# Windowed attention on one core: the first loads issued at once by GpSimd, a quarter of the first q over SyncE, TensorE's loop without alignment

## Chip, core and metric

One core of one Trainium2 chip. The metric is the device time of one execution in microseconds (us). A single core has no second die to compare with, so only the spread of the runs themselves says what noise is. The experiments came in five sets, each on another chip, and beside each set nine runs of the kernel before were taken: these 45 runs lie between 942.4 and 944.6 us, and their five medians between 942.6 and 943.1 us. Differences of less than about 0.5 us between two medians are therefore not read as anything here.

## The reference

Attention inside windows of 64 rows, in float32 arrays of 4 x 4096 x 1536:

```python
logits = np.einsum('bnwd,bnud->bnwu', q_w, k_w) * D ** -0.5     # nw = 64 windows of W = 64 rows
logits = logits - logits.max(axis=-1, keepdims=True)
attn = np.exp(logits)
attn = attn / attn.sum(axis=-1, keepdims=True)
out = np.einsum('bnwu,bnud->bnwd', attn, v_w)
```

Every byte of q, k and v is read once and every byte of out written once: 302 MB and 101 MB.

## The kernel before

The kernel works in 32 units of 512 rows. For each unit GpSimd issues three loads (q, k, v), which cast float32 to float16 on the way and land in one of two landing buffers each, and one store. It copies a landed tile to its working place, tells TensorE through a semaphore, and requests the same tile of two units later. So loads are queued two units, about 55 us, ahead. The parts that matter:

```python
def hand_over(x, u, dst, m, g):                # GpSimd, for each tile of units 1 to 31
    gp.wait_ge(landed[x][u % NL], ...)         # the transfer has landed
    gp.wait_ge(m, u)                           # the working tile is free
    gp.tensor_copy(out=dst[...], in_=landing[x][u % NL][...]).then_inc(c_l, 1)
    ...
    gp.sem_inc(g, 1)                           # TensorE may go
    request(x, u + NL)                         # next load into the landing buffer
# [...]
# start: q of unit 0 comes as float32 over SyncE in four pieces, GpSimd casts it
for lo, hi, c0, c1, s in (
    (0, 1, 0, D // 2, d_r0), (0, 1, D // 2, D, d_r1), (1, 2, 0, D, d_r2), (2, SLOTS, 0, D, d_r3)
):
    nc.sync.dma_start(out=outs[0][:, lo:hi, c0:c1], in_=raw[:, lo:hi, c0:c1]).then_inc(s, 16)
nc.gpsimd.wait_ge(d_r0, 16)
nc.gpsimd.affine_select(out=ident[:, :], ...).then_inc(i_p, 1)
load("k", 0, k16, d_k0)
load("v", 0, v16, d_v0)
for i in range(SLOTS):
    nc.gpsimd.wait_ge((d_r1, d_r2, d_r3, d_r3)[i], 16)
    nc.gpsimd.tensor_copy(out=q16[:, i, :], in_=outs[0][:, i, :]).then_inc(c_q, 1)
    if i == 1:
        request("q", 1)
for x, u in (("k", 1), ("v", 1), ("q", 2), ("k", 2), ("v", 2)):
    request(x, u)
# [...]
with nc.Fori(0, N, engines=OrderedEngineSet([PE]), head_slot={PE: 0}):   # loop head at slot 0 of a fetch block
    tensor_unit()
# [...]
for u in range(1, N):
    hand_over("q", u, q16, m_q, g_q)
    hand_over("k", u, k16, m_k, g_k)
    gp.wait_ge(m_q, u + 1)
    store(u - 1)
    hand_over("v", u, v16, m_v, g_v)
```

The softmax here doesn't subtract the row's maximum and nothing guards it: scores larger than these inputs give would overflow.

## Time and profile before

| | before |
|---|---|
| time, median of the first three runs | 943.18 us (942.78 to 943.63) |
| span of the profiled run | 941.3 us |
| busiest compute engine | TensorE, 70% |

How to read the views: PE is TensorE (PEld its weight loads, PEq its sequencer), DVE VectorE, ACT ScalarE, POOL GpSimd. DMA queue q0 carries what GpSimd issues, q1 what SyncE issues. A line of the timeline has its start in us, its length in us, the engine, the line of the source, the operation, what it wrote and read, and in brackets how long the engine was idle before it and what ended that. In the view of narrow stretches the last two columns are the mean busy share of the 16 DMA engines and the GB/s that they moved, counted in SBUF bytes. The prediction below shows the lines of the kernel before.

### The profile page before, as it was taken

What the parts mean: (1) busy time and instruction counts of PE and PEld (TensorE: products, weight loads), DVE (VectorE), ACT (ScalarE), POOL (GpSimd) and SP (SyncE); (2) the same over time, 40 slices, a digit from 0 to 9 for tenths busy, and PEclk for the clock granted to TensorE, in tenths of its full rate; (3) what the DMA queues carried; (4) which work ended last, traced back from release to release, by engine and by line L of the source; (5) the groups of instructions that cost most, each with busy time, mean ns of one, the idle gap of its engine ahead of it and who ended that gap; (6) DMA issues with size and microseconds to landing.
All of it is one profiled execution on the core that took longest, in us unless ns stands there. A gap on an engine that the chain in (4) does not pass through costs nothing. (4 is left out here: it accounts for less than half of the span.)

```text
span 941.3 us, 11422 instructions
## 1 busy us (share of the span) xinstructions
PE 655.5 (70%) x4096; PEld 395.4 (42%) x3456; DVE 279.8 (30%) x453; ACT 335.9 (36%) x642; POOL 340.4 (36%) x228
## 2 busy tenths in 40 slices
PE   1888676866777768677677686776767768667672
PEld 1555344533455334444244543444433445334440
DVE  0433322333313323133332233322333223332231
ACT  1444433333333333333433324433333323343332
POOL 4344333344333443333423334333343333433221
PEclk9999978889878888888888878978888888898887
DMA  9999999999999999999999999999999999999998
GB/s 247 216 217 281 254 247 281 282 281 263 239 280 283 281 271 232 280 282 281 277 234 273 281 281 282 238 264 282 280 282 248 253 284 279 281 257 245 283 297 366
DMA packets 27084, 253.35 MB, mean 269 GB/s; under 512 B 2112, under 2 KB 2112, under 8 KB 10688
## 3 DMA queue, kind: packets, MB, share of 16 engines
q0 software_dynamic: 26208, 246.95, 100.0%
q1 hardware_dynamic: 864, 6.29, 1.7%
q14 instruction: 10, 0.08, 0.0%
q8 instruction: 2, 0.03, 0.0%
HBM read 301.99 MB, written 100.66 MB: 428 GB/s over the span
## 5 line engine op out<-in xcount | busy, mean ns | idle before, releaser
L157 PE MATMUL lt<-xq,xk 128*128 128x256 f16 x1536 | 215.5, 292 | 0.0
L145 PE MATMUL tp<-ident,k 128*128 128x128 f32 x768 | 149.1, 339 | 84.8 <-PEq L211 74.7
L294 POOL COPY v<-vl 128x3072 f32<-128x3072 f32 x31 | 85.2, 2747 | 296.0 <-DMA vl<-in_v_dram 296.0
L157 PEld LDWEIGHTS lt<-xq,xk 128*128 128x128 f16 x1536 | 159.6, 104 | 33.0
L145 PEld LDWEIGHTS tp<-ident,k 128*128 128x128 f32 x768 | 115.5, 176 | 104.7 <-issue 102.1
L145 PE MATMUL tp<-ident,q 128*128 128x128 f32 x768 | 109.7, 289 | 71.1 <-DVE xq L220 37.0
L220 ACT COPY xk<-tp 128x512 f32<-128x512 f32 x96 | 59.3, 618 | 264.0 <-ACTq L211 264.0
L186 PEld LDWEIGHTS <-et 128*128 128x128 f16 x384 | 34.5, 108 | 283.0 <-issue 277.2
L145 PEld LDWEIGHTS tp<-ident,q 128*128 128x128 f32 x768 | 89.2, 148 | 111.0 <-issue 110.4
L220 DVE COPY xk<-tp 128x512 f32<-128x512 f32 x96 | 66.5, 693 | 229.0 <-DVEq L211 229.0
L294 POOL COPY q<-ql 128x3072 f32<-128x3072 f32 x31 | 85.0, 2742 | 109.9 <-DMA ql<-in_q_dram 109.9
L294 POOL COPY k<-kl 128x3072 f32<-128x3072 f32 x31 | 85.2, 2747 | 107.6 <-DMA kl<-in_k_dram 107.6
L113 PE MATMUL o<-v,et 128*128 128x512 f16 x384 | 113.6, 440 | 0.0
L113 PE MATMUL sp<-ones,et 128*128 128x1 f16 x256 | 25.7, 170 | 116.6 <-PEq L211 114.3
L262 ACT ACTIVATE et<-lt,zeros 32x128 f16<-32x128 f32 x256 | 92.0, 360 | 39.4 <-ACTq L211 36.2
L220 ACT COPY xq<-tp 128x512 f32<-128x512 f32 x96 | 59.8, 623 | 122.1 <-ACTq L211 122.1
L249 DVE TENSOR_SCALAR out<-o,rs 128x512 f32<-128x512 f32 x128 | 91.1, 747 | 33.6 <-DVEq L211 29.6
L273 ACT ACTIVATE out<-tp,rs 128x512 f32<-128x512 f32 x64 | 44.0, 687 | 139.7 <-ACTq L211 112.9
L220 DVE COPY xq<-tp 128x512 f32<-128x512 f32 x96 | 66.3, 690 | 90.0 <-DVEq L211 89.8
L113 PE MATMUL tp<-v,et 128*128 128x512 f16 x256 | 91.9, 446 | 0.0
L239 DVE RECIPROCAL rs<-sp 128x2 f32<-128x2 f32 x64 | 10.7, 168 | 264.8 <-DVEq L211 264.8
L113 PE MATMUL lt<-v,et 128*128 128x512 f16 x128 | 58.3, 456 | 0.0
(21 smaller groups left out, 224.0 us busy)
## 6 DMA issues: line engine op xcount, KB each, us to landing
out_dram<-out POOLq DMA_DIRECT2D x31, 3072.0 KB, 61.8
ql<-in_q_dram POOLq DMA_DIRECT2D x31, 1536.0 KB, 54.9
kl<-in_k_dram POOLq DMA_DIRECT2D x31, 1536.0 KB, 54.9
vl<-in_v_dram POOLq DMA_DIRECT2D x31, 1536.0 KB, 54.9
out_dram<-out SPq DMA_DIRECT2D x2, 1536.0 KB, 9.7
out<-in_q_dram SPq DMA_DIRECT2D x1, 1536.0 KB, 13.9
k<-in_k_dram POOLq DMA_DIRECT2D x1, 1536.0 KB, 13.1
v<-in_v_dram POOLq DMA_DIRECT2D x1, 1536.0 KB, 19.7
```

What stands on the lines that cost most here:

```text
L113: return nc.tensor.add_instruction(mybir.InstMatmult(name=nc.get_next_instruction_name(), engine=PE, ins=[low(rhs), low(w)], outs=[low(o)] ...
L145: ins = nc.tensor.transpose(tps[g % 2][:, r, j, :], pairs[:, c * P : (c + 1) * P], ident[:, :])
L157: ins = nc.tensor.matmul(lts[h][:, r, :, :], lhsT=halves(xk, c)[:, r, h, :, w], rhs=halves(xq, c)[:, :, h, :, w], start=(c == 0 and w == 0 ...
L186: ld = nc.tensor.ldweights(w)
L220: copy(out=dst, in_=tps[g % 2][:, :, :, :]).then_inc(f_c[g % 4], 1)
L239: ve.reciprocal(out=rs[:, n : n + R], in_=sp[:, n : n + R]).then_inc(n_d, 1)
L249: ins = ve.tensor_scalar_mul(scaled(u, n, j), bank(n, j), scalar1=rs[:, n : n + 1])
L262: ins = sc.activation(ets[h][s, :, :, s], lts[h][s, :, :, s], EXP, bias=zeros[s, 0:1], scale=scale)
L273: ins = sc.activation(scaled(u, n, j), bank(n, j), COPY, bias=0.0, scale=rs[:, n : n + 1])
L294: gp.tensor_copy(out=dst[:, :, :].bitcast(FP32), in_=landing[x][u % NL][:, :, :].bitcast(FP32)).then_inc(c_l, 1)
```

## The change

The intent: nothing at the start should wait for anything it does not need. GpSimd no longer waits for the first piece of q before it issues k and v; three quarters of q come by a casting load of GpSimd itself, only a quarter over SyncE, which saves three of four casts. The alignment of TensorE's loop is dropped in the same step.

```diff
-        for lo, hi, c0, c1, s in (
-            (0, 1, 0, D // 2, d_r0), (0, 1, D // 2, D, d_r1), (1, 2, 0, D, d_r2), (2, SLOTS, 0, D, d_r3)
-        ):
-            nc.sync.dma_start(out=outs[0][:, lo:hi, c0:c1], in_=raw[:, lo:hi, c0:c1]).then_inc(s, 16)
+        first = rows(qf, 0, SLOTS, SLOTS)
+        nc.sync.dma_start(out=outs[0][:, 0, :], in_=first[:, 0, :D]).then_inc(d_r0, 16)
+        nc.gpsimd.dma_start(
+            out=q16[:, 1:, :].rearrange("p r d -> p (r d)"), in_=first[:, 0, D:]
+        ).then_inc(d_q0, 16)
+        load("k", 0, k16, d_k0)
         ...
-        nc.gpsimd.wait_ge(d_r0, 16)
         nc.gpsimd.affine_select(...)
-        load("k", 0, k16, d_k0)
         load("v", 0, v16, d_v0)
-        for i in range(SLOTS):
-            nc.gpsimd.wait_ge((d_r1, d_r2, d_r3, d_r3)[i], 16)
-            nc.gpsimd.tensor_copy(out=q16[:, i, :], in_=outs[0][:, i, :]).then_inc(c_q, 1)
-            if i == 1:
-                request("q", 1)
-        for x, u in (("k", 1), ("v", 1), ("q", 2), ("k", 2), ("v", 2)):
-            request(x, u)
+        for u in (1, 2):
+            for x in "qkv":
+                request(x, u)
+        nc.gpsimd.wait_ge(d_r0, 16)
+        nc.gpsimd.tensor_copy(out=q16[:, 0, :], in_=outs[0][:, 0, :]).then_inc(c_q, 1)
         ...
-        with nc.Fori(0, N, engines=OrderedEngineSet([PE]), head_slot={PE: 0}):
+        with nc.Fori(0, N, engines=OrderedEngineSet([PE])):
         ...
-        sy.wait_ge(c_q, SLOTS)
-        sy.sem_inc(g_q, 1)
+        sy.wait_ge(c_q, 1)
+        sy.sem_inc(g_q, 1)._wait_ge(d_q0, 16)
```

More of the change, by code (lines that the diff above doesn't have):

```diff
@@ L72 @@
     sp = ps("sp", [P, 4])
-    d_r0, d_r1, d_r2, d_r3, d_k0, d_v0 = (
-        sem(n) for n in ("d_r0", "d_r1", "d_r2", "d_r3", "d_k0", "d_v0")
-    )
+    d_r0, d_q0, d_k0, d_v0 = (sem(n) for n in ("d_r0", "d_q0", "d_k0", "d_v0"))
     landed = {x: [sem(f"d_{x}{i + 1}") for i in range(NL)] for x in "qkv"}
@@ L302 @@
     with tc.tile_critical(no_gpsimd_drain=True):
-        raw = rows(qf, 0, SLOTS, SLOTS).rearrange("p h (r d) -> p (h r) d", d=D)
-        for lo, hi, c0, c1, s in (
-            (0, 1, 0, D // 2, d_r0), (0, 1, D // 2, D, d_r1), (1, 2, 0, D, d_r2), (2, SLOTS, 0, D, d_r3)
-        ):
-            nc.sync.dma_start(
-                out=outs[0][:, lo:hi, c0:c1], in_=raw[:, lo:hi, c0:c1]
-            ).then_inc(s, 16)
+        first = rows(qf, 0, SLOTS, SLOTS)
[4 more added lines that the diff above has]
+        load("k", 0, k16, d_k0)
         nc.vector.memset(ident[:, :], 0.0).then_inc(i_d, 1)
         nc.gpsimd.wait_ge(i_d, 1)
-        nc.gpsimd.wait_ge(d_r0, 16)
         nc.gpsimd.affine_select(
```

## The prediction

> **What bounds the kernel now.** I read the page first, then the DMA queues, the GpSimd timeline, narrow stretches of the start and of the end, and last the waits of TensorE. The page says at once which resource never rests:
>
> ```profile
> PE 655.5 (70%) x4096; PEld 395.4 (42%) x3456; DVE 279.8 (30%) x453; ACT 335.9 (36%) x642; POOL 340.4 (36%) x228
> ...
> DMA  9999999999999999999999999999999999999998
> ...
> q0 software_dynamic: 26208, 246.95, 100.0%
> q1 hardware_dynamic: 864, 6.29, 1.7%
> q14 instruction: 10, 0.08, 0.0%
> ...
> HBM read 301.99 MB, written 100.66 MB: 428 GB/s over the span
> ```
>
> The row of the DMA engines is at nine tenths or more in 39 of 40 slices, from the first to the last but one, while the busiest compute engine has 30% to spare. The GB/s row counts bytes as SBUF sees them: a load that casts float32 to float16 counts half of what it reads from HBM. So 216 GB/s in such a row means 432 GB/s read from HBM, and the row's ups and downs (216 to 283) are the mix of loads and stores, not idle time.
>
> The GpSimd timeline gives the beat, because GpSimd copies each landed tile as soon as it lands:
>
> ```profile
> 7.61 0.68 POOL L106 DMA_DIRECT2D k<-in_k_dram  x1 [0.25 <-issue]
> ...
> 16.26 2.87 POOL L324 CAST q<-out 128x1536 f16<-128x1536 f32 x2 [3.88 <-DMA out<-in_q_dram]
> ...
> 35.33 2.75 POOL L294 COPY q<-ql 128x3072 f32<-128x3072 f32 x1 [13.20 <-DMA ql<-in_q_dram]
> ...
> 42.65 2.75 POOL L294 COPY k<-kl 128x3072 f32<-128x3072 f32 x1 [3.44 <-DMA kl<-in_k_dram]
> ...
> 130.14 2.75 POOL L294 COPY v<-vl 128x3072 f32<-128x3072 f32 x1 [10.06 <-DMA vl<-in_v_dram]
> ```
>
> The copy of v of unit 4 starts at 130.14 us and that of unit 31, the last, at 918.13 us in the same timeline: 788.0 us for 27 units, 29.18 us a unit, or 7.30 us for each of its four transfers (q, k, v in, out back) of 3.15 MB of HBM traffic each, 431 GB/s. All 128 transfers at that beat are 934 us of the 941.3 us span. What is left, some 7 us, is all that a change of the start or the end can act on.
>
> The start and the end in narrow stretches (columns: stretch, length, busy time of PE, PEld, DVE, ACT and POOL with counts, granted clock, DMA share, GB/s):
>
> ```profile
> 1.00:2.00 1.00, 0.00 (x0) 0.00 (x0) 0.74 (x5) 1.00 (x1) 0.00 (x0) 1.00 0.10 9
> 2.00:3.00 1.00, 0.00 (x0) 0.00 (x0) 0.00 (x0) 0.49 (x2) 0.00 (x0) 1.00 1.01 123
> 3.00:4.00 1.00, 0.00 (x0) 0.00 (x0) 0.00 (x0) 0.00 (x0) 0.00 (x0) 1.00 0.92 349
> 4.00:5.00 1.00, 0.00 (x0) 0.00 (x0) 0.00 (x0) 0.00 (x0) 0.00 (x0) 1.00 1.12 412
> ...
> 10.00:11.00 1.00, 0.00 (x0) 0.00 (x0) 0.00 (x0) 0.00 (x0) 1.00 (x2) 1.00 1.89 283
> 11.00:12.00 1.00, 0.00 (x0) 0.00 (x0) 0.00 (x0) 0.00 (x0) 1.00 (x2) 1.00 0.52 135
> 12.00:13.00 1.00, 0.00 (x0) 0.00 (x0) 0.00 (x0) 0.00 (x0) 0.39 (x1) 1.00 0.97 197
> 13.00:14.00 1.00, 0.00 (x0) 0.00 (x0) 0.00 (x0) 0.00 (x0) 0.00 (x0) 1.00 0.87 184
> ...
> 20.00:21.00 1.00, 1.00 (x6) 1.00 (x6) 0.23 (x1) 0.00 (x0) 1.00 (x3) 1.00 1.04 215
> ```
>
> The reader should see three things. Bytes flow from about 1.9 us, so the DMA engines are not kept waiting by GpSimd's late first issue at 7.61 us: SyncE's q fills that time. There is a seam at 10 to 19 us, where q ends and the casting loads of k begin: 135 to 233 GB/s there against 215 steadily after. And TensorE's first work at 19.54 us, although it looks like the prize, sits on nothing: the DMA engines are already full.
>
> TensorE waits rather than limits:
>
> ```profile
> PE sp L113 <- PEq L211: 114.3, 29, 4.5
> PE tp L145 <- PEq L211: 108.2, 53, 19.5
> ```
>
> Its sequencer stands in waits for v (first line) and for q or k (second) for 222 us, 19.5 of them before unit 0, so about 6.5 us a unit of slack. At the end it is the same: the last v lands at 918 us, compute is over at 929 us, and the DMA share stays near 1 until 937 us, working off two earlier stores and then the last one.
>
> **What the Trainium skill says.** "DMA: Bandwidth & Descriptors", section "Issuing engines are not separate DMA queues": transfers started from sync and from gpsimd run on the same 16 DMA engines, and a second issuer saves only issue time. [...] Same page, "Specifications": fabric ceiling 435 GB/s; the 431 GB/s measured here is 99% of it, so I allow no faster steady beat. Same page, "Queues, rings and completion order": an engine goes round robin between queues by packet; a narrow SyncE piece beside GpSimd's stream should then finish in about twice its lone time; this trace has only a hint, SyncE's last half of q landing 13.9 us after its issue, once k had joined. "Runtime: NRT & Kernel Launch", section "Instruction fetch mechanics": instructions come in blocks of 256 and a taken branch outside the resident window costs a fetch. The trace before has 10 instruction packets on q14 in all, so no fetch per round; what an unaligned loop does, no run shows yet.
>
> **The change part by part.**
> 1. *Bytes.* Unchanged from HBM: q of unit 0 is still 3.15 MB read. Three quarters of it (2.36 MB) go as casting loads at 431 instead of plain loads at 414 GB/s: 5.70 us becomes 5.48, a gain of 0.2 us.
> 2. *First bytes.* SyncE's first piece is still issued at 0.95 us and flows at 1.9. It is 0.79 MB, about 1.9 us of the engines alone. GpSimd's first issue moves from 7.61 to about 1 us; with 0.6 to 0.7 us for an issue and about a microsecond to the first packet its bytes flow from about 2.7 us, before SyncE's are used up. So no hole. The slow first two slices (123 and 349 instead of 431 GB/s, 0.39 MB, 0.9 us) stay.
> 3. *The seam.* It goes, since one queue streams from the start. Its price before: 11 to 19 us moved 135+197+184+221+197+233+197+197 = 1561 of the 8 x 215 = 1720 KB that steady state moves, 0.7 us; and in the q stretch and the slice 10 to 11 something more. A check from the other side: the copy of q of unit 1, the fourth transfer, starts at 35.33 us. Less 4 x 7.30 that is an effective start of 6.1 us. Of it, 1.9 us is first issue to first bytes, about 1.8 us a constant lag of landing behind moving (k's bytes are all counted by 19.0, and it lands at 7.61 + 13.1 = 20.7), so 2.4 us was lost. Of these 0.9 stay by point 2. Gain 1.5 us, with the 0.2 of point 1 inside it.
> 4. *GpSimd's own work.* Three of four casts of q (2.90 and 2.87 us for two each) are gone, 4.3 us; the remaining one is 1.45 us. Nine issues at about 0.62 us end at some 6.7 us, so the cast ends near 8.5, before the rest of q lands (near 11.5). TensorE starts near 12 instead of 19.54. All this is off the path, worth 0.
> 5. *TensorE's alignment.* One round is 4096/32 = 128 matmuls and 3456/32 = 108 weight loads by the page, and 29 semaphore and loop instructions by the built program: 265, over one block of 256, so aligned or not it touches two blocks for nearly every start. I expect no new fetches. If there were one a round, a few us would go into the 6.5 us of slack, and 31 blocks of 16 KB are 0.5 MB or 1.2 us of DMA time.
>
> Sum: 943.2 - 1.5 (seam and plain loads) - 0.3 (a choice: SyncE and GpSimd together may also fill the slice from 3 to 4 us better) = 941.4. The other parts are 0.
>
> **Rivals.**
> - *The start counts in full*: TensorE starts 7.5 us earlier, and so ends 7.5 us earlier: 935.7. For it: nothing but the timeline of TensorE. Against: bytes flow from 1.9 us in both kernels, and the last v cannot land before 96 loads and the stores between them have passed at 7.30 us each. I give it little.
> - *Nothing is gained*: the seam's loss is a cost of warming up, not of the two queues, and appears again in the first casting loads: 943. For it: the slices from 13 to 19 us are at 184 to 233 GB/s with GpSimd's queue nearly alone. Chance one in five.
> - *GpSimd's queue fills*: nine issues outstanding against the 7 to 8 of steady state (54.9 us to landing by 7.30). It would block in an issue until the first load lands, the cast then delays TensorE to some 13 us; still before k at about 18.5: 941.4 all the same.
> - *TensorE loses its instructions each round*: hidden as in point 5, plus at most 1.2 us of DMA: 942.6. Only a stall of more than 6.5 us each round would show as more, and then as much as 31 us for each further microsecond.
>
> **Range and chances.** 941.4 us; 939.6 to 942.9 should hold it eight times in ten: 1.8 us below for a lag or ramp that also shrinks (all 2.4 plus the noise of 0.8 between runs), 1.5 above for the second and fourth rival. 2% are 18.9 us, nearly three times the whole 7 us that are not steady transfers: faster by 2% has 0.3%, slower by 2% only through the last rival, 1%.
>
> **What would show it.** Copies of q of unit 1 starting at 33.5 us instead of 35.33, of the last v near 916.3 instead of 918.13, with the same 29.18 us a unit between: then the gain arose in the first 30 us and was kept. The seam of 10 to 19 us should read 210 to 220 GB/s. TensorE's first matmul near 12 us with its waits longer by some 7 us in unit 0 and 1 would show that its start is worth nothing. Instruction packets still about ten would settle the alignment. I am wrong if the beat itself changes from 29.18, if the DMA share shows a hole at 2 to 4 us, or if the queue of instructions grows by hundreds of packets.

## The result

943.39 us (median of four runs, 943.12 to 943.52) against 943.0 us before (four runs, 942.78 to 943.63). The ratio is 1.0002, 95% interval 0.9987 to 1.0017: the same. (That of the two medians is 1.0004.) The prediction was 941.4, within 939.6 to 942.9, and was wrong: the gain of 1.8 us is not there.

The page of the changed kernel is nearly the page of before: SyncE's queue q1 holds less, and the instruction queue q8 has one packet where before has two (the last line below is before's).

```profile
DMA  9999999999999999999999999999999999999998
...
q0 software_dynamic: 26352, 248.13, 100.5%
q1 hardware_dynamic: 432, 3.93, 1.1%
q14 instruction: 10, 0.08, 0.0%
q8 instruction: 1, 0.02, 0.0%
...
q8 instruction: 2, 0.03, 0.0%
```

The start did what was expected. From TensorE's timeline, and GpSimd's with the copies of q of units 1 and 3, of k of unit 3 and of v of units 3 and 31:

```profile
12.46 5.57 PE L143 MATMUL tp<-ident,q 128*128 128x128 f32 x24 [12.46 <-PEq L209]
```

```profile
34.05 2.75 POOL L292 COPY q<-ql 128x3072 f32<-128x3072 f32 x1 [25.23 <-DMA ql<-in_q_dram]
...
77.76 2.74 POOL L292 COPY q<-ql 128x3072 f32<-128x3072 f32 x1 [3.21 <-DMA ql<-in_q_dram]
86.12 2.75 POOL L292 COPY k<-kl 128x3072 f32<-128x3072 f32 x1 [4.47 <-DMA kl<-in_k_dram]
...
100.72 2.74 POOL L292 COPY v<-vl 128x3072 f32<-128x3072 f32 x1 [10.02 <-DMA vl<-in_v_dram]
...
918.53 2.74 POOL L292 COPY v<-vl 128x3072 f32<-128x3072 f32 x1 [10.56 <-DMA vl<-in_v_dram]
```

The same before (TensorE's first matmuls, then the copies; that of q of unit 1 stands in the prediction):

```profile
19.54 3.68 PE L145 MATMUL tp<-ident,q 128*128 128x128 f32 x16 [19.54 <-PEq L211]
...
79.05 2.74 POOL L294 COPY q<-ql 128x3072 f32<-128x3072 f32 x1 [3.20 <-DMA ql<-in_q_dram]
86.33 2.75 POOL L294 COPY k<-kl 128x3072 f32<-128x3072 f32 x1 [3.40 <-DMA kl<-in_k_dram]
...
100.96 2.75 POOL L294 COPY v<-vl 128x3072 f32<-128x3072 f32 x1 [9.91 <-DMA vl<-in_v_dram]
...
918.13 2.74 POOL L294 COPY v<-vl 128x3072 f32<-128x3072 f32 x1 [10.55 <-DMA vl<-in_v_dram]
```

TensorE starts at 12.46 us instead of 19.54. The copy of q of unit 1 starts 1.28 us earlier than before (34.05 against 35.33). The lead is still 1.29 us at 77.76. At the very next tile it is 0.21 us, and at the last v it is a loss of 0.40 us. In this pair of profiles the gain arrived, lived for 78 us, and was lost in lumps. The first and largest lump is at k of unit 3: 8.36 us from the copy before (77.76 to 86.12), where before has 7.28. That is the last load ahead of the first store.

**A finer look at the same traces.** The skill's page "DMA: Bandwidth & Descriptors", section "Why a DMA increments its semaphore by 16 and not by 1", says that each of the 16 engines of a transfer adds 1 when its own share has landed. The traces agree: 16 increments a transfer, spread over some us. So each landing can be read as 16 arrival times. "Last" is what the kernel waits for, "mid" their median (us, from the trace's semaphore events):

```
                 before          before again    changed         changed again
                 mid    last     mid    last     mid    last     mid    last
q of unit 1      33.95  35.28    32.82  34.60    32.46  33.99    32.51  33.92
v of unit 3      99.60 100.91    98.55 100.52    98.41 100.66    98.55 100.44
v of unit 31    916.29 918.07   915.28 918.12   915.07 918.47   915.20 918.72
```

In the first pair of profiles the mid engine keeps its lead to the end (916.29 - 915.07 = 1.22 us), while the last engine gives all of it back: its distance to the mid one grows from 1.53 to 3.40 us. In all 20 profiles the span ends 23.2 to 23.4 us after the last arrival of v of unit 31, so that arrival sets the time. The middle does not: at v of unit 31 it is 1.0 us later in "before" than in "before again" (916.29 and 915.28), and the last arrivals agree to 0.05 us. The columns "again" belong to the first experiments, and they already warn that a single profile of "before" was no good measure of the start.

### The profile page after: what moved, and what is told of

Read it like the earlier page. It is cut to its first block, busy times and chain, and to the rows that moved or that the text cites. A ratio compares the mean times of both kernels' runs of the same rounds, so it can differ in the third digit from the quotient of the medians. Undisturbed runs are those within 1.5% of the kernel's fastest.

```text
span 941.7 us, 11415 instructions
## 1 busy us (share of the span) xinstructions
PE 659.9 (70%) x4096; PEld 402.3 (43%) x3456; DVE 279.6 (30%) x453; ACT 335.5 (36%) x642; POOL 337.3 (36%) x226
## 5 line engine op out<-in xcount | busy, mean ns | idle before, releaser
L155 PE MATMUL lt<-xq,xk 128*128 128x256 f16 x1536 | 218.0, 295 | 0.0
L143 PE MATMUL tp<-ident,q 128*128 128x128 f32 x768 | 116.8, 302 | 68.3 <-PEq L209 34.8
L143 PEld LDWEIGHTS tp<-ident,q 128*128 128x128 f32 x768 | 94.7, 155 | 110.3 <-issue 109.6
L111 PE MATMUL o<-v,et 128*128 128x512 f16 x384 | 109.5, 428 | 0.0
L111 PE MATMUL tp<-v,et 128*128 128x512 f16 x256 | 89.7, 437 | 0.0
```

The lines of the kernel that those rows point to most:

```text
L111: return nc.tensor.add_instruction(mybir.InstMatmult(name=nc.get_next_instruction_name(), engine=PE, ins=[low(rhs), low(w)], outs=[low(o)] ...
L143: ins = nc.tensor.transpose(tps[g % 2][:, r, j, :], pairs[:, c * P : (c + 1) * P], ident[:, :])
L155: ins = nc.tensor.matmul(lts[h][:, r, :, :], lhsT=halves(xk, c)[:, r, h, :, w], rhs=halves(xq, c)[:, :, h, :, w], start=(c == 0 and w == 0 ...
```

## The experiments

Theory A: the 16 DMA engines are 16 separate queues that never rest, each with the same bytes; a delay of one is never made up, and the one with the most delay sets the end. Theory B: chance of one execution. Theory C: the unaligned loop costs what the loads gain. More theories came up on the way and are named in the expectations. "Lost at the first store" is, for the last engine, the time from q to v of unit 3 less 21.87 us, which is three transfers at 7.29 us. The edits are shortened to the lines that matter; declarations of semaphores and waits that only follow from them are left out.

### 1 and 2: both kernels again

No edit.

> The changed kernel once more, unaltered. Each of the 16 DMA engines adds 1 to a transfer's semaphore when its share has landed; the trace of the changed kernel shows that the middle one of the 16 kept a lead of 1.2 us over the kernel before to the end, while the last one lost 0.65 us near 80 us, 0.5 near 230 us and 0.5 near 903 us. Theory A (16 queues that never rest, and the slowest decides: small delays of single engines eat the gain): the first copies are again 1.3 us earlier, the middle engine keeps over 1 us to the end, the last engine loses it in lumps; the time is 943.1 to 943.6. Theory B (pure chance in one profiled execution): the lumps are at other places, and some execution shows 941.5 to 942.5.

> The kernel before once more, unaltered, with its own profile. Theory A: the last engine stands 1.3 us behind the middle one from the first casting load on, and 1.8 or less at the end; 942.8 to 943.4. Theory B (chance): its lag at the end may be anything from 1.3 to 3.5 us, as far from its first profile as the changed kernel is. Ratio 1.000.

Measured: the changed kernel 943.37 us (942.85 to 943.74), before 943.06 us (942.57 to 943.36); beside them nine more runs of before, median 942.6 us. The expectation for the start failed: "again" the lead at q of unit 1 is only 34.60 - 33.92 = 0.68 us. The loss at the first store came back at the same place (0.94 us after 1.08), and before lost 0.33 us there after 0.04. The lag of before at the end was 2.84 us, not the 1.8 or less that A expected, so part of B holds too: the size of the last engine's lag at the end varies between executions of one and the same kernel. What does not vary much is the last arrival of v of unit 31: 918.07, 918.12, 918.47, 918.72.

### 3 and 4: the two parts alone

```diff
 # 3: the changed kernel with
-        with nc.Fori(0, N, engines=OrderedEngineSet([PE])):
+        with nc.Fori(0, N, engines=OrderedEngineSet([PE]), head_slot={PE: 0}):
 # 4: the kernel before with the opposite edit
```

> The new loads with the loop of TensorE aligned as before. Theory A: the loads alone bring the first copies 1.3 us forward, and the last engine gives most of it back; 942.8 to 943.5. Theory C (the unaligned loop costs what the loads gain, through an instruction fetch late in the first round): the loads alone keep their gain: 941.7 to 942.2, and no fetch of 16 KB near 36 us.

> The old loads with the loop of TensorE not aligned. Theory A: no more than one fetch of 16 KB at another time, which moves one of the 16 DMA engines by 0.7 us; 942.8 to 943.7. Theory C: the alignment is worth 1.0 to 1.5 us by itself: 944.0 to 944.5.

Measured: loads alone 943.39 us (942.98 to 943.77), alignment alone 943.40 us (942.77 to 943.43). The loads do not gain without the alignment change, so C falls. With the aligned loop a 16 KB instruction packet came at 142, 200 and 85 us in three profiles, with the unaligned one at 36, 37 and 42 us. It took 0.95 to 0.97 us each time, and there was one such packet in the loop's run, not one a round. In the changed kernel it is seen to hit one engine. Before it, 12 of the 16 arrivals stand within 0.2 us of the mid one and the other four at 0.23, 0.31, 0.45 and 1.54 us behind it (q of unit 1). After it these four are still there, and one of the 12 stands 1.15 us behind and stays. So the engine lost about 1.1 us, a little more than the packet took, not the 0.7 us that the expectation names. This is theory A in small.

A rival stays here. With the aligned loop there is one more 16 KB packet, at 3.6 to 4.7 us, which takes 1.0 to 1.5 us; all four profiles with the aligned loop have it and none of the other 16. So part of the start's gain may come from the dropped alignment and not from the loads: with the old loads the last arrival of q of unit 1 is at 35.28 and 34.60 us aligned and 33.95 us unaligned, with the new loads at 34.36 us aligned and 33.99 and 33.92 us unaligned. One profile each of numbers 3 and 4 does not settle it.

Over the three profiles of each kind, the last engine at q of unit 1 is at 35.28, 34.60, 33.95 us (mean 34.61) with the old loads and 33.99, 33.92, 34.36 us (mean 34.09) with the new. The start's gain is 0.5 us, not 1.3 (for the mid engine 33.13 and 32.52 us, 0.6 us). At the first store the old loads lose 0.04, 0.33, 0.38 us, the new 1.08, 0.94, 0.84 us: 0.7 us more. Numbers 7 and 9 below are two more profiles of the new start, because their extra copies flow only from 96 us on: they have q of unit 1 at 33.64 and 33.72 us and lose 0.72 and 0.37 us. With them the start gains 0.7 us and the first store costs 0.5 us more. The two are of one size, and their difference is within the spread of the profiles.

### 5 and 6: the whole start held back

```diff
+        nc.vector.memset(xk[:, 0:2, :], 0.0).then_inc(w_s, 1)      # 6: xk[:, :, :]
+        nc.sync.wait_ge(w_s, 1)
+        nc.gpsimd.wait_ge(w_s, 1)
         first = rows(qf, 0, SLOTS, SLOTS)
```

> The changed kernel with nothing but its start held back by about 1.1 us: SyncE and GpSimd wait for one more memset of VectorE (128x1024 float32) before their first transfers. In the six profiles so far a group of load packets is stretched at 81 to 83.5 us, where the engines turn from loads to the first store: by 6.5 to 8.0 us summed over the 16 engines with the new loads, 0.2 to 3.0 with the old ones, less the later the engines arrive there. Theory D (something at a fixed time of the execution holds the first store up): the delay is swallowed there; the stretch falls to 0 to 3 us and the end moves by 0.4 us or less: 943.2 to 943.8. Theory E (the turn from loads to stores costs the same whenever it comes): stretch 6 to 8 us, end later by 1.1 us: 944.2 to 944.8.

> The same with the start held back by about 3.3 us (memset of 128x3072). Theory D: about 0.9 of it is swallowed at the first store: 945.4 to 946.0, no stretch left at 84 to 87 us. Theory E: 946.3 to 946.9, with the stretch of 6 to 8 us moved to 84.5 to 87 us. If the time moves by less than 2 us, then the start is not on the path at all, against my account of the end as the start plus 128 transfers.

Measured: 944.47 us (944.15 to 944.90) and 946.95 us (946.67 to 947.13). SyncE's first transfer went out at 2.18 and 4.32 us instead of 0.95 us, so it was held back by 1.2 and 3.4 us; against 943.37 us of the changed kernel the ends came 1.1 and 3.6 us later. A delay of the whole start, for all engines alike, is paid in full. (In the first of the two the last arrival of q of unit 1 moved by only 0.2 us, 33.99 to 34.21, and that of v of unit 31 by 1.2 us: the last engine at one early landing is no measure of the end either.) The loss at the first store did not shrink (1.25 and 1.21 us), and the stretched packets moved with the start, to 84.3 us in the second. Theory D falls, E holds. So the start is on the path, as the prediction said; what it said wrongly is how much of it the change takes away.

### 7: a few more bytes on every engine, by mistake

```diff
             for a in range(2):
                 sy.sem_inc(fr[a], 1)
+            e = u - NO
+            if e:
+                sy.wait_ge(d_x, 16 * e)
+            at = (N - 1) * UR + 3 * e
+            sy.dma_start(
+                out=of[at : at + 3, :1536], in_=qf[3 * e : 3 * (e + 1), :1536]
+            ).then_inc(d_x, 16)
+        sy.wait_ge(d_x, 16 * (N - NO))
```

> The changed kernel with 29 small extra copies on SyncE, one a unit, of 3 rows of 6144 bytes each from q to rows of out that the last store overwrites: three rows give three of the 16 DMA engines 29 x 6144 bytes more, 6.6 us at the 27 GB/s of one engine. Theory A (16 separate full queues, the slowest sets the end): the end moves by nearly that, less the up to 3 us by which those three may stand ahead of the slowest: 947 to 950.5, and three of the 16 counts of each landing fall behind step by step. Rival F (the engines share the work, so only bytes count): 29 x 18.4 KB at 431 GB/s, 1.2 us: 944.2 to 945.

Measured: 945.01 us (944.88 to 945.32). The trace shows why the experiment failed as meant: SyncE's queue has 464 = 29 x 16 pieces of 1152 bytes. Three whole rows are contiguous and were spread over all 16 engines. Read as what it was, it helps all the same: each engine got 29 pieces of 0.064 us, 1.86 us, and the end came 1.6 us later than in the changed kernel. Little of it, if any, was hidden.

### 8: a first store early

```diff
+        nc.gpsimd.wait_ge(i_p, 1)
+        nc.gpsimd.dma_start(out=of[0:P, 0:P], in_=ident[:, :]).then_inc(d_w, 16)
         load("v", 0, v16, d_v0)
```

> The changed kernel with one early store of the identity (64 KB) into rows of out that the store of unit 0 overwrites later, issued by GpSimd after the load of k. Theory G (the first write to HBM of the execution costs the 0.85 to 1.1 us that the last engine loses at 81 to 83.5 us): that loss is paid early or not at all, the stretch at the first real store falls under 2 us, 942.4 to 942.9. Theories D and E: stretch as before, 6 to 8 us, and the time 943.3 to 943.8, a little later for the extra transfer (0.15 us).

Measured: 943.24 us (942.90 to 943.72), and 1.16 us lost at the first real store. Theory G falls: the loss is not the price of the first write.

### 9: three engines held up

```diff
+            for e in range(2 * (u - NO), 2 * (u - NO) + 2):
+                if e:
+                    sy.wait_ge(d_x, 16 * e)
+                at = (N - 1) * UR + 3 * e
+                sy.dma_start(
+                    out=of[at : at + 3, :1152], in_=qf[3 * e : 3 * (e + 1), :1152]
+                ).then_inc(d_x, 16)
+        sy.wait_ge(d_x, 32 * (N - NO))
```

> The earlier try with three engines spread itself over all 16 (its records show 464 pieces of 1152 bytes on SyncE's queue, not 87 of 6144), since whole rows are contiguous. Now two copies a unit, 58 in all, of 3 rows of 4608 bytes, which do not join: three engines get 58 x about 0.175 us (4608 bytes at the rate of 6144 in 0.234 us) = 10.2 us more each, the other 13 nothing. Theory A (16 separate full queues, the slowest sets the end): later by 10.2 less the up to 3 us by which they may stand ahead: 950.5 to 953.5, and three of the 16 counts of a landing fall behind step by step. Rival F (only the sum of bytes counts): 802 KB at 431 GB/s, 1.9 us: 945 to 945.6.

Measured: 952.68 us (952.43 to 953.02), 9.3 us later than the changed kernel and 9.6 us later than the kernel before beside it, for 174 pieces (58 a row, 4608 bytes, 0.191 us each: 11.1 us on each of three engines). GpSimd's timeline, v of unit 31:

```profile
927.59 2.74 POOL L293 COPY v<-vl 128x3072 f32<-128x3072 f32 x1 [10.70 <-DMA vl<-in_v_dram]
```

The arrivals of that transfer, in us from the mid one, show three engines far behind and thirteen about where the changed kernel has all of its own (up to 3.40 us behind); the mid one arrives at 915.39 us, where the changed kernel has 915.07:

```
-0.31 -0.29 -0.27 -0.22 -0.20 -0.17 -0.16 -0.08  0.08  0.19  1.75  2.47  2.80 10.48 11.96 12.14
```

This is the clearest result. 802 KB, which spread evenly would cost 1.9 us by calculation, cost 9.3 us; number 7, whose 534 KB did spread evenly, cost 1.6 us. Rival F falls and A holds: the engines do not help each other, and the slowest sets the end. The view of the last stretches shows it from the other side:

```profile
930.00:935.00 5.00, 4.47 (x28) 0.86 (x11) 2.47 (x6) 1.93 (x4) 0.34 (x1) 1.00 0.26 108
935.00:940.00 5.00, 1.07 (x5) 0.10 (x1) 2.10 (x3) 1.79 (x3) 0.00 (x0) 0.93 0.78 329
```

A mean DMA share of 0.26 at the end of a kernel whose page shows a full queue: most engines have run out of work, and the kernel waits for three. The kernel before, for comparison:

```profile
930.00:935.00 5.00, 0.00 (x0) 0.00 (x0) 0.00 (x0) 0.00 (x0) 0.00 (x0) 0.57 1.00 424
```

### 10 to 12: what makes the first store dear

Three theories (H: where GpSimd's descriptor ring stands, that is, how many loads it issued before; I: GpSimd's early issue; J: q as plain copies or casts).

```diff
 # 10: the changed kernel, all of the first q as float32 over SyncE in two pieces, four casts
+        for lo, s in ((0, d_r0), (2, d_q0)):
+            nc.sync.dma_start(out=outs[0][:, lo : lo + 2, :], in_=first[:, lo : lo + 2, :]).then_inc(s, 16)
 # 11: the kernel before with one small load of GpSimd ahead of the first k
+        nc.gpsimd.dma_start(out=xk[:, 0, :P], in_=qf[:P, :P]).then_inc(d_x, 16)
 # 12: the changed kernel, all of the first q as one casting load of GpSimd
+        load("q", 0, q16, d_q0)
```

> The changed kernel, but all of the first q over SyncE as float32 (two pieces, four casts on GpSimd, as before), GpSimd's loads issued at once. What of the new loads makes the turn to the first store dearer (last engine +0.84 to 1.24 us in six runs with new loads, +0.02 to 0.36 in three with old)? Theory H (where GpSimd's descriptor ring stands: one more casting load ahead of that turn): like the old, 0 to 0.4. Theory I (GpSimd's early issue): 0.8 to 1.25. Theory J (the first q as plain float32 copies or as casts): 0 to 0.4. Time 942.6 to 943.4 under H and J, 943.2 to 943.8 under I.

> The kernel before with one small load more (128x128 float32, 64 KB, 0.15 us) issued by GpSimd ahead of the first k, so that its descriptor ring stands where it stands in the changed kernel. Theory H: the last engine loses 0.8 to 1.25 us at the first store, time 943.5 to 944.1. Theories I and J: 0 to 0.4, time 942.7 to 943.4.

> All of the first q as one casting load of GpSimd, nothing on SyncE, no cast on GpSimd. H, I and J all say 0.8 to 1.25 us at the first store. The start: nothing flows until GpSimd's issue, about 0.6 us later than SyncE's, so the first k should land 0.3 to 0.7 us later than in the changed kernel, and the end too: 943.6 to 944.2. If the end is not later, the start of the first bytes is not what counts.

Measured: 943.50 us with 0.02 us lost at the first store, 943.32 us with 0.02 us, 944.10 us with 0.94 us. H and I fall (11 and 10 lost nothing), but the time of 943.50 us is not in the 942.6 to 943.4 us that went with sparing the turn. Number 12 was later by 0.7 us than the changed kernel, as expected of first bytes that wait for GpSimd's issue. J was left standing.

### 13 to 18: plain copies, their size, their queue, their number

```diff
 # 13: half of q over SyncE          14: the changed kernel and 16 pieces of 12288 bytes over SyncE
+  out=outs[0][:, :2, :], in_=first[:, 0, : 2 * D]
+                                    out=outs[0][:16, 2:, :], in_=first[:16, 0, 2 * D :]
 # 15: all of q plain float32, in two pieces, on GpSimd's queue
+  nc.gpsimd.dma_start(out=outs[0][:, lo : lo + 2, :], in_=raw[:, lo : lo + 2, :])
 # 16: the quarter in two transfers of half a row each
+  for c, s in ((0, d_r0), (D // 2, d_r1)): nc.sync.dma_start(out=outs[0][:, 0, c : c + D // 2], ...)
 # 17: the changed kernel and 16 pieces of 512 bytes over SyncE
+  nc.sync.dma_start(out=outs[0][:16, 3, :P], in_=first[:16, 0, :P]).then_inc(d_x, 16)
 # 18: half of q in two transfers of a quarter each
+  for i, s in enumerate((d_r0, d_r1)): nc.sync.dma_start(out=outs[0][:, i, :], ...)
```

> The changed kernel with half of the first q over SyncE (pieces of 12288 bytes, two casts on GpSimd) instead of a quarter (pieces of 6144). Theory K (plain pieces of 12288 bytes, the size of a store's, spare the turn): the last engine loses 0 to 0.4 us at the first store, the start keeps its lead, and this is the best version: 942.4 to 943.2. Theory L (the amount: all of q has to be plain): 0.4 to 1.0 us lost, 943.0 to 943.6.

> The changed kernel and one small load more on SyncE, 16 pieces of 12288 bytes, one for each DMA engine (0.46 us each). K: 0 to 0.4 us lost at the first store, which pays for the load: 943.0 to 943.6. L: 0.8 to 1.2 lost, 943.6 to 944.1.

> All of the first q as plain float32, two pieces, but issued by GpSimd, nothing on SyncE. If plain copying spares the turn: 0 to 0.4 us lost at the first store. If SyncE's queue does it (theory M): 0.8 to 1.25. The start is 0.6 us later than with SyncE, as in r12: 943.4 to 944.0 under K or L, 944.0 to 944.6 under M.

> The changed kernel with SyncE's quarter of q in two transfers (half a row each) on two semaphores. Theory N (two or more transfers of SyncE at the start spare the turn): the last engine loses 0 to 0.4 us at the first store, time 942.5 to 943.3. If it loses 0.7 to 1.25, N falls and the cause of the dear turn stays open: 943.2 to 943.8.

> The changed kernel and a second transfer on SyncE of 16 pieces of 512 bytes. N: 0 to 0.4 us lost at the first store, 942.6 to 943.4. If r14's load worked by its bytes or its 0.46 us for each engine: 0.7 to 1.25, 943.2 to 943.8.

> Half of q over SyncE in two transfers of a quarter each. N: 0 to 0.4 us lost, and with the early start of r13 (last engine at v of unit 0 at 26.3 us) the best version of all: 942.4 to 943.1. If N is wrong: as r13, 0.8 lost, 943.3 to 943.6.

Measured, with all others for comparison (last column the median time; "SyncE" the number of transfers that SyncE issues at the start; "lost" the first store's loss of the mid and the last engine; then the arrivals of v of units 3 and 31):

```
kernel                        SyncE   lost         v of unit 3     v of unit 31     time
                                      mid   last   mid    last     mid    last
before                          4     0.06  0.04   99.60 100.91   916.29 918.07   943.18
before again (2)                4     0.13  0.33   98.55 100.52   915.28 918.12   943.06
alignment only (4)              4     0.18  0.38   98.44  99.91   915.22 918.35   943.40
old loads, small one more (11)  4     0.02  0.02   99.71 101.00   916.56 917.98   943.32
all q by SyncE (10)             2     0.14  0.02   98.45  99.35   915.07 918.14   943.50
small plain load more (14)      2     0.05  0.04   99.36 100.98   916.22 918.79   944.23
quarter in two (16)             2     0.11  0.04   98.52  99.55   915.25 917.77   943.21
tiny second transfer (17)       2     0.22  0.62   98.49 100.10   915.20 918.14   943.42
half in two (18)                2     0.23  0.23   98.59  99.66   915.30 918.77   943.53
changed                         1     0.40  1.08   98.41 100.66   915.07 918.47   943.39
changed again (1)               1     0.49  0.94   98.55 100.44   915.20 918.72   943.37
loads only (3)                  1     0.36  0.84   98.52 100.78   915.19 917.96   943.39
early store (8)                 1     0.51  1.16   98.73 100.72   915.47 917.84   943.24
half of q by SyncE (13)         1     0.46  0.81   98.56 100.18   915.23 918.57   943.43
small copies on all (7)         1     0.38  0.72   98.50  99.94   916.68 920.03   945.01
small copies on three (9)       1     0.50  0.37   98.64  99.67   915.39 927.53   952.68
start 1 us later (5)            1     0.55  1.25   99.79 101.77   916.46 919.69   944.47
start 3 us later (6)            1     0.61  1.21  101.92 103.73   918.56 921.87   946.95
q by GpSimd alone (12)          0     0.37  0.94   99.46 100.84   916.28 919.70   944.10
q plain by GpSimd (15)          0     0.49  0.69   99.54 100.93   916.18 919.48   944.66
```

J, K and L all fail against this list. Number 15 has all of q plain and loses 0.69 us, number 13 has pieces of 12288 bytes and loses 0.81 us, number 14 has a small second transfer of SyncE and loses 0.04 us. What sorts the 20 rows without overlap, for the mid engine, is the number of transfers on SyncE at the start (theory N): two or more lose 0.02 to 0.23 us, none or one 0.36 to 0.61 us. For the last engine it is 0.02 to 0.62 against 0.69 to 1.25 us, with one exception, number 9 with 0.37 us. Number 16, the strictest test (the same bytes, on the same queue, cut in two), went from about 1 us to 0.04 us. Number 17, at 0.62 us, missed the 0.4 us that N expected. So N is a rule that fits, with two weak points, and why the count should matter 80 us later is not known. One rival was not tested: the number of pieces on SyncE's queue at the start sorts the rows just as well (144 or more against 128 or fewer), since every second transfer here also brought more pieces.

As versions to be faster, these six failed: number 18, which N called the best of all at 942.4 to 943.1 us, took 943.53 us. Numbers 14 and 15, at 944.23 and 944.66 us, were slower than any of their theories allowed, and 0.8 and 1.3 us slower than the changed kernel; in both the mid engine is about 1 us late already at v of unit 3.

The list also says what the first store's loss is worth: nothing that is seen at the end. Numbers 10, 16 and 18 are spared it and have v of unit 3 at 99.35 to 99.66 us, 1.0 to 1.3 us ahead of the changed kernel. Their times are 943.50, 943.21 and 943.53 us. Between units 3 and 31 the last engine needs 818.2 to 819.1 us there, against 817.2 to 818.4 us in the rows of before, changed and their parts. The arrivals show where the lead goes. In number 16 the last engine is 1.08 us behind the mid one at v of unit 4, 1.56 at k of unit 5, 2.16 at k of unit 9 and 2.49 at k of unit 31; in number 10 it is 1.09, then 1.47 at k of unit 5, 1.84 at k of unit 7, 2.09 at k of unit 9, 2.46 at k of unit 14 and 2.98 at k of unit 31. In every unit from the third on, k is the last load ahead of a store. Over 18 profiles (all but 7 and 9) this distance grows by more than 0.12 us between two landings 77 times: 68 times at k, 9 times at v, never at q, and it never shrinks by as much. So the first turn to a store is no special case: what it spares, later turns can take. GpSimd's timeline of number 16 puts the two ends side by side:

```profile
99.61 2.74 POOL L293 COPY v<-vl 128x3072 f32<-128x3072 f32 x1 [10.03 <-DMA vl<-in_v_dram]
...
917.83 2.74 POOL L293 COPY v<-vl 128x3072 f32<-128x3072 f32 x1 [10.53 <-DMA vl<-in_v_dram]
```

None of the 18 runs beats the kernel before, whose nine-run medians beside the five sets of runs were 942.6, 942.65, 943.12, 942.94 and 942.98 us.

## Why the prediction was wrong, point by point

**What bounds the kernel: right.** The DMA engines, from 1.9 us to the end. Holding the start back by 1.2 and 3.4 us moved the end by 1.1 and 3.6 us (5, 6), 1.86 us of extra work on each engine moved it by 1.6 us (7), and TensorE's 7 us earlier start moved it by nothing. One comparison does not carry what it was used for: the 431 GB/s are bytes on the HBM side, while the skill's page "DMA: Bandwidth & Descriptors", section "Specifications", gives the ceiling of 435 GB/s for the SBUF side, where the casting loads move 216 GB/s. The beat held all the same. The first rival, 935.7 us, fell as foreseen.

**Points 2, 4, 5 of the change: right in kind.** (Point 1, 0.2 us, was not measured by itself.) GpSimd's issues ended at 7.33 us (6.7 expected), its one cast at 8.8 us (8.5), and TensorE started at 12.46 us ("near 12"). The instruction packets were not to grow and did not: q14 kept its ten, and q8, which the prediction did not look at although the 16 KB packets are there, went from two to one. Point 2 had GpSimd's first bytes at 2.7 us; its first packet starts at 4.34 us, because about 2.9 us passed between issue and first packet and not the 1 us that SyncE needed. SyncE's pieces start until 5.83 us, so there was still no hole at 2 to 4 us, as the narrow stretches of the changed kernel show:

```profile
2.00:3.00 1.00, 0.00 (x0) 0.00 (x0) 0.00 (x0) 0.49 (x2) 0.93 (x3) 1.00 0.72 160
3.00:4.00 1.00, 0.00 (x0) 0.00 (x0) 0.00 (x0) 0.00 (x0) 1.00 (x3) 1.00 1.03 418
4.00:5.00 1.00, 0.00 (x0) 0.00 (x0) 0.00 (x0) 0.00 (x0) 1.00 (x3) 1.00 1.31 333
...
14.00:15.00 1.00, 0.87 (x5) 0.50 (x4) 0.39 (x1) 0.48 (x1) 0.00 (x0) 1.00 0.93 197
```

The slice from 3 to 4 us does fill better, 418 instead of 349 GB/s, which is 0.16 us at 431 GB/s; but GpSimd's queue has not started then, so the 0.3 us called a choice came true by half and not for its reason. And the packets of the kernel before show that GpSimd's queue started at 10.03 us there: nothing was in use beside SyncE's queue at 8 to 10 us.

**Point 3, the seam: the step that failed first.** The seam itself went: 11 to 19 us moved 1749 KB in the changed kernel, against 1561 before and 1720 in steady state. The point's own first count of it, 0.7 us, was of the right size. The "check from the other side", from one copy of one profile, put 1.5 us in its place. That copy's time is the arrival of the last of 16 engines, and so is the landing of k from which the "constant lag" of 1.8 us was read: k's mid engine arrives at 19.35 us and the last at 20.70. In three profiles of the old loads it was 35.28, 34.60 and 33.95 us, a spread of 1.3 us between executions that all end within 0.3 us of each other in those traces. The profile that I had was the latest of the three. Averaged, the new loads win 0.5 us there (0.7 with numbers 7 and 9), a third to a half of the term of the sum.

**"The gain is kept to the end": the step that failed second.** The prediction looked for a beat of 29.18 us a unit and found it, and it concluded that a lead, once won, stays. For the mid engine the beat is indeed the same: from v of unit 3 to v of unit 31 it takes 816.69 us before and 816.66 us in the changed kernel. But what counts is the last of 16 engines, and its lead can be lost at single events: at the first store (0.7 us more than with the old loads in the mean of three and three, 0.5 with numbers 7 and 9) and at later turns to a store, mostly by 0.2 to 0.6 us each. The prediction treated the DMA engines as one server; they are 16, and run 9 shows what that means.

**The rivals and the range.** "Nothing is gained" came true with a chance of one in five, but not for its reason: it named a cost of warming up that would reappear in the first loads, and the first loads did land earlier. The range ended at 942.9 us, just short of the 943 us of this rival, although I gave it one in five; losses after the start had no more room than the 1.2 us of the instruction packets. The 2% classes were right (same).

**What stays open.** Why the first turn from loads to a store mostly costs the last engine about 1 us with none or one transfer of SyncE at the start and little with two or more; and why the turns after it cost anything. A lead of 1 us at unit 3 (10, 16) is lost at those later turns; whether another engine becomes the last one there is not shown, because the traces do not name the engine of an arrival. How the start's gain divides between the loads and the dropped alignment is open too.

## What to carry to other kernels

A saturated DMA queue is 16 queues: read the last of a transfer's 16 arrivals beside the middle one before a start, an end or a hiccup is given a number, because an even cost on all engines and a cost on a few differ by a factor (1.6 us for 534 KB on all, 9.3 us for 802 KB on three here). When the whole expected gain is under 0.3% of a kernel, one profile of each version cannot show it: take the profile of before twice and see how far two executions of one kernel differ at the very line the estimate rests on. And small strided copies on few partitions or rows, put somewhere "for free" on another queue, may be the dearest in the kernel, as the 58 copies of number 9 were.

## What the Trainium skill lacked or had wrong

- "DMA: Bandwidth & Descriptors" says of bulk loads beside other traffic that they run at the pace of their slowest engine, but has no number for uneven work over a long full queue. Here 802 KB on three engines moved the end by 9.3 us; spread evenly they are 1.9 us at the 431 GB/s of this kernel.
- The same page warns that the copy is split over up to 16 engines by its slowest dimension. It mentions splitting a contiguous single-dimension pattern; the runs show it for whole rows too: 3 rows of 6144 bytes became 16 pieces of 1152 bytes, and 3 rows of 4608 bytes out of 6144 stayed 3 pieces.
- No page has the cost of the first turn from loads to stores: in these runs 0.02 to 1.25 us for the last engine, mostly sorted by the number of SyncE's transfers at the start, cause unknown. Later turns cost the last engine mostly 0.2 to 0.6 us at a time.
- "Runtime: NRT & Kernel Launch" says that a taken branch outside the resident window costs a fetch. It does not say that a fetch also takes its time from one DMA engine: a packet of 16 KB took 0.95 us, and one of the 16 arrivals stayed about 1.1 us later from then on. For the loop of 265 instructions no fetch a round was seen, aligned (two packets of 16 KB in all) or not (one).
